# Attention's combining cut finer, two loads doubled earlier, one normalising moved, in a hybrid decoder block on one Trainium2 core

## Chip, cores and metric

One core of one Trainium2 chip runs the whole program. The metric is device time in microseconds (us) of an execution; the figures before are the median of three runs. The engines are TensorE (PE: matmuls; PEld: its weight loads), VectorE (DVE), ScalarE (ACT), GpSimd (POOL) and SyncE (SP), which here only issues DMA transfers.

## The reference

For x of 2048 tokens by 1024 channels, in fp32:

```
h = rmsnorm(x);  proj = h @ w_in                  # q, k, v, u, z, gate_a, gate_b
q, k = rope(q), rope(k);  u, z = gelu(u), gelu(z)
for g in 3 patterns (dilation 1, 4, 16), 4 heads of 64 each:
    o_g, lse_g = windowed attention of 128 keys back
y_attn = sum_g softmax_g(lse) * o_g               # 2048 x 256
y_gmlp = u * (tril(w_spatial) @ layernorm(z) + b) # chunks of 128 tokens, 4 groups
merged = sigmoid(gate_a) * (y_attn @ w_branch_attn) + sigmoid(gate_b) * (y_gmlp @ w_branch_gmlp)
x = x + rmsnorm(merged @ w_out)
h = rmsnorm(x);  x = x + rmsnorm(relu(h @ w_mlp_in)^2 @ w_mlp_out)
```

## The kernel before

Every matmul operand is split into a high part and a remainder, and each product is three matmuls of 128 x 128 by 512 columns (`mm3`); some large products use a seven-product scheme over halves of the operands. Tokens go in chunks c = 0..3 of 512, and in two halves (c = 2, 3 first).

PE's order is the order in which the program is written. The order on the other engines is made by a planner from estimated times; `behind()` pins what is written inside it behind the last instruction written before it on each engine (behind that one only). Each engine then works through its queue in that order, so an instruction that waits holds all that are behind it.

The stretch that the change touches is the middle of the program. A generator (`filler`, advanced by `steps(n)`) gives PE work in steps of three matmuls: the products for u, z and the gates. Around it the code places other work by counting steps.

- `gates()` (line 681) runs the gate products, `seq` of places t, four steps (12 matmuls) each. The last phase (product i = 4 of the first half of tokens) has ten places, from t = LAST; LAST starts at step 34 after the end of attention, LAST+j at step 34 + 4j. At the end of each place the code issues on SP the store of the previous place's result (line 745), then one transfer of the list `ins` (line 748), two at some places, and then evicts the place's PSUM bank with DVE (lines 755 to 769). Four PSUM banks serve the products in turn. In the last phase `ins` holds the operands of the next products: the chunk c = 0 of h (`hT_b`, six 512 KB transfers, of which the first two are rows that ACT and DVE split at LAST+4 and LAST+7, line 716) and the second half of the z weights (`w_z`).
- Attention leaves per pattern an output and its maximum and sum in DRAM (`att_d`). `combine(c)` (line 985) loads the three patterns of a chunk (`A`, three transfers of 528 KB on SP), computes the softmax weights on small tiles (DVE, with one exponential on ACT), multiplies the first pattern's output by its weight (16 small operations on ACT) and the other two (two large products on DVE), adds the three (two large additions on DVE), transposes the sum on PE and stores it (`ya`). It is a generator in five parts. `combined(...)` places the parts of the chunks c = 2, 3, 0 at counted steps during the gate products: loads at steps 0, 4 and 20, weights at 10, 26 and 42, products at 13, 29 and 46, additions at 19, 34 and 49, transposes at 32, 50 and 69. Chunk c = 1 goes through the z products behind (`todo`, line 1116).
- After the gates come the z products of chunks 0 and 1 (`z_chunk`, line 582): eight steps per 128 tokens, a gelu on ACT, statistics on DVE; at the end of a chunk a root on ACT (`rstd_of`, line 103) and four DVE operations that normalise z (line 597).
- Then `load_y` (line 1157) loads the branch operands `yt` (six tiles, split into high part and remainder: four on POOL, two by ACT and DVE, lines 74 and 82), `early_gates` loads gates and the first rows of w_out, and `merge` (line 1197) runs the branch products: 18 matmuls for each of eight dt, evicted by DVE with the gates (line 1211). After dt = 0 and dt = 1 `spatial_out` runs the spatial product of z (`sz`, line 565): chunk 0's after dt = 0, chunk 1's after dt = 1.

Of the kernel before, what the change touches and what calls it, by code (L numbers as in the profile page):

```python
# [9 lines left out]
F32 = mybir.dt.float32  # L10
# [7 lines left out]
P = 128  # L18
# [18 lines left out]
def widen(ap, n):  # L37

    return bass.AP(tensor=ap.tensor, offset=ap.offset, ap=[list(z) for z in ap.ap] + [[0, n]])
# [3 lines left out]
def block_kernel(ctx, tc, a, out):  # L43
# [59 lines left out]
    def rstd_of(pl, ss, n, scale, tag):  # L103

        r = pl.tile([P, n], F32, name=f"r_{tag}", tag=f"rs_r{n}")
        act.activation(r, ss, AF.Sqrt, bias=eps, scale=scale)  # L106
        v = pl.tile([P, n], F32, name=f"v_{tag}", tag=f"rs_v{n}")
        dve.tensor_scalar(v, ss, scale, EPS, op0=OP.mult, op1=OP.add)
        dve.reciprocal(r, r)  # L109
        t = pl.tile([P, n], F32, name=f"t_{tag}", tag=f"rs_t{n}")  # L110
        if n == 1:
            dve.scalar_tensor_tensor(t, r, v, r, op0=OP.mult, op1=OP.mult)  # L112
        else:
            dve.tensor_mul(t, r, r)
            dve.tensor_mul(t, t, v)
        dve.tensor_scalar(t, t, -0.5, 1.5, op0=OP.mult, op1=OP.add)  # L116
        dve.tensor_mul(r, r, t)  # L117
        return r
# [462 lines left out]

    def z_chunk(zp, ws, c):
        zt = zp.tile([P, 4, 512], F32, name=f"z_{c}", tag="z", bufs=2)
        mv = sm.tile([P, 4, 2], F32, name=f"mv_{c}", tag="mv")
        for i in range(4):
            p = psum_mm(f"z_{c}{i}")
            yield from steps_tok(ws, c, i, p)
            if i == 2 and late and c > 1:
                sz_out(*late.pop(0))
            act.activation(zt[:, i, :], p, AF.Gelu_apprx_tanh)  # L590
            bs = sm.tile([P, 6], F32, name=f"bs_{c}{i}", tag="bs")
            dve.bn_stats(bs, zt[:, i, :])
            dve.bn_aggr(mv[:, i, :], bs)
        r = rstd_of(sm, mv[:, :, 1], 4, 1.0, f"ln{c}")
        for i in range(4):
            z = zt[:, i, :]
            dve.tensor_scalar(z, z, mv[:, i, 0:1], r[:, i:i + 1], op0=OP.subtract, op1=OP.mult)
        late.append((zp, zt, c))

    queue = [(9, "u", 0, 1), (10, "u", 1, 1), (11, "z", 0, 1), (12, "z", 1, 1)]  # L600
    queue += [(13, "g", 0, 1)]
    queue += [(11, "z", 0, 0), (12, "z", 1, 0)]
# [78 lines left out]
    def gates():  # L681
# [14 lines left out]
        for t, (half, i, n) in enumerate(seq):  # L696
            if t in starts:
                ph, t0 = starts[t], t
                if ph + 1 < len(phases):
                    s = (ph + 1) % 2  # L700
                    if not slots[s]:
                        slots[s] = hp.tile([P, 2, 2, 4, 512], F32R, name="opA", tag="hT", bufs=2)
                    for j, i2 in enumerate(phases[ph + 1][1]):
                        new = operand(phases[ph + 1][0], i2, slots[s][:, j])
                        ins += new[0]
                        todo += new[1]
                else:
                    hs = reload_h(0)
                    h0 = f32(hT[0])
                    rows = [(h0[:, 1, k:k + 2], hT_d[0][:, k:k + 2]) for k in (0, 2)]  # L710
                    ins += rows + ws[4:6] + hs[4:6] + ws[6:] + hs[6:]
                    todo += [(hT[0], 0), (hT[0], 2)]
            elif todo and (t - t0) % 3 == 1 and t > t0 + 1:
                w, k = todo.pop(0)
                with behind():
                    split(w[:, 0, k:k + 2], w[:, 1, k:k + 2], f32(w)[:, 1, k:k + 2], "act",
                          "pool" if t < LAST else "dve")
            if t == LAST - 4:
                ws = want(5)
                ins += ws[:4]  # L720
            if t == LAST:
                g_["ends"] = g_["vs"] + zs[8:]
            for n_ in (t + PIECES,) if t < LAST else {0: (4, 5), 1: (6, 7), 2: (8,), 3: (9,)}.get(t - LAST, ()):
                piece(n_ if t < LAST else LAST + n_)
            split_piece(t + SPLITS)
            if i in (1, 6, 5, 4):
                bank[n] = psum_mm(f"g{half}{i}{n}")
            p, w, h = bank[n], g_["w"].pop(t), g_["b"][half, i]
            for k in range(4):
                for m, (l, r) in enumerate(((0, 0), (0, 1), (1, 0))):  # L730
                    pe.matmul(p, w[:, l, k], h[:, r, k], start=i in (1, 6, 5, 4) and not k and not m,  # L731
                              stop=k == 3 and m == 2, skip_group_check=True)
                if (t, k) == (3, 2) and late:
                    sz_out(*late.pop(0), zs[4:8])
                yield
            if t == 3:
                a = [ga.tile([P, 512], F32, name=f"ga{n_}", tag=f"ga{n_}", bufs=1) for n_ in range(12)]
                xs += a[:7]
                zs += a[7:9]
                vs = a[9:11]  # L740
                g_["vs"] = vs + xs[8:] + zs[8:]
                g_["raws"] += a[11:]
            x, z, fn = xs[n], zs[n], AF.Copy if n < 8 else AF.Gelu_apprx_tanh
            while out_:
                sp.dma_start(*out_.pop())
            for _ in range(2 if half and i == 4 or t in (LAST + 5, LAST + 7) else 1):
                if ins:
                    sp.dma_start(*ins.pop(0))
            if i == 1:
                act.activation(x, p, AF.Copy)  # L750
            elif i == 2:
                act.activation(z, p, fn)
                o = z, 0, 0
            elif i == 6:
                dve.tensor_add(z, x, p)
            elif i == 7:
                dve.tensor_add(x, x, p)
            elif i == 5:
                if (half, n) == (0, 0):
                    g_["vs"] = a[9:11]  # L760
                v = g_["vs"].pop(0)
                g_["vs"].append(v)
                dve.tensor_add(v, x, p)  # L763
                o = v, 1, 1
            elif i == 3:
                dve.tensor_add(z, z, p)
                o = z, 0, 1
            else:
                dve.tensor_add(x, x, p)
                o = x, 1, 0  # L770
            if n > 7 and i in (5, 3, 4):
                act.activation(o[0], o[0], fn)
            if i in (2, 5, 3, 4):
                c, dst = 2 * half + o[2], gate_d if n < 8 else u_d
                out_.append((dst[n % 8 * 2 + o[1], :, c * 512:(c + 1) * 512], o[0]))
# [209 lines left out]
    def combine(c):  # L985
# [10 lines left out]
        for g in range(3):  # L996
            dve.tensor_sub(E[:, :, g, :], A[:, :, g, 260:264], M)
        act.activation(E, E, AF.Exp, scale=0.125)
        Z = sm.tile([P, 4, 3, 4], F32, name=f"Z_{c}", tag="cZ")
        for g in range(3):  # L1000
            dve.tensor_mul(Z[:, :, g, :], E[:, :, g, :], A[:, :, g, 256:260])
# [3 lines left out]
        for g in range(3):  # L1005
            dve.tensor_mul(E[:, :, g, :], E[:, :, g, :], M)
        yield
        for i in range(4):
            for j in range(4):
                o = A[:, i, 0, j * 64:(j + 1) * 64]  # L1010
                act.activation(o, o, AF.Copy, scale=E[:, i, 0, j:j + 1])
        for g in range(1, 3):
            o = A[:, :, g, 0:256].rearrange("p i (j e) -> p i j e", j=4)
            dve.tensor_tensor(o, o, widen(E[:, :, g, :], 64), op=OP.mult)
        yield
        dve.tensor_add(A[:, :, 1, :256], A[:, :, 1, :256], A[:, :, 2, :256])
        dve.tensor_add(A[:, :, 0, :256], A[:, :, 0, :256], A[:, :, 1, :256])
        yield
        for m in range(2):
# [60 lines left out]
    def combined(*order):  # L1080
        for n, k in order:
            steps(n)
            with behind():
                next(cs[k])

    combined((0, 0), (4, 1), (6, 0), (3, 0), (6, 0), (1, 2), (6, 1), (3, 1), (3, 0), (2, 1),
             (8, 2), (4, 2), (3, 2), (1, 1), (19, 2))
    steps(75 - 69)
    ec.close()
    ega.close()  # L1090
# [22 lines left out]
        steps(1)  # L1113
    for k in range(3):
        load_wb(k)
    todo = {9: (3,), 34: (3,), 36: (3,), 39: (3,), 60: (3,)}
    for n in range(1, 62):
        steps(1)
        if zin:
# [37 lines left out]
    def load_y(c, engs=(("act", "dve"),)):  # L1157
        cs = slice(c * 512, (c + 1) * 512)
        yt = [bot.tile([P, 2, 512], F32R, name=f"yt{c}{k}", tag=f"yt{k}") for k in range(6)]
        for k in range(6):  # L1160
            split_in(yt[k], ya_d[k, :, cs] if k < 2 else yg_d[k - 2, :, cs], None, *engs[k % len(engs)])
        return yt
# [505 lines left out]

    ttp = None
    yt = load_y(2, (("pool", "pool"),) * 4 + (("act", "dve"),) * 2)  # L1670
    early_gates(2)
    mg = merge(2, yt, {}, spatial_out)
    for n, c in enumerate(chunks):
# [414 lines left out]
```

## Time and profile before

| | us |
|---|---|
| median of three runs | 2584.74 (2582.64 to 2586.54) |
| the profiled execution | 2587.89, its span 2586.2 |
| PE busy | 2546.1 |
| DVE busy | 1695.6 |
| POOL busy | 1385.4 |
| ACT busy | 1271.9 |

The profile is of one execution. Its times are counted from the start of the span. A busy PE is not PE at its peak: the time between the starts of two matmuls tells how fast it works, and the granted clock which of its two levels it has. An idle time in brackets names what ended it.

### The profile page before, as it was taken

The numbers are of one execution on the slowest core, as the hardware profiler recorded it, in microseconds if no ns is written. First come the engines' busy times: TensorE is split into PE (matmuls) and PEld (weight loads), VectorE is DVE, ScalarE is ACT, GpSimd is POOL, SyncE is SP. The second block draws the span as 40 slices with busy tenths as digits, with TensorE's granted clock in tenths as the row PEclk, the third lists the DMA queues.
The fourth block names the chain that finished last, engine by engine and source line by source line (L and its number), as shares of the span: only waits on it lengthen the run. The fifth ranks groups of instructions, "written<-read, shape, count | busy, mean of one in ns | idle before, by whom it ended". The sixth has DMA issues, their size and how long they took to land. (4 is left out here: it accounts for less than half of the span.)

```text
span 2586.2 us, 36297 instructions
## 1 busy us (share of the span) xinstructions
PE 2546.1 (98%) x12122; PEld 2125.5 (82%) x12122; DVE 1695.6 (66%) x3063; ACT 1271.9 (49%) x2696; POOL 1385.4 (54%) x1385
## 2 busy tenths in 40 slices
PE   9999999999999999999999999999999999999998
PEld 8888888888888887788887788888778888888886
DVE  5676575445443447777767678778787777767766
ACT  5213211154446434544445645665447776766755
POOL 0363354274545555311113858787887767767634
PEclk9999999999999999999999999999999999999999
DMA  8779778989897899877766766467884222122235
GB/s 313 284 246 325 254 244 278 308 246 296 264 329 218 239 287 326 279 263 266 272 225 240 249 204 212 145 194 215 259 258 143 90 90 89 51 90 90 90 125 201
DMA packets 413293, 568.73 MB, mean 220 GB/s; under 512 B 58929, under 2 KB 247601, under 8 KB 412082
## 3 DMA queue, kind: packets, MB, share of 16 engines
q1 hardware_dynamic: 387600, 504.73, 59.8%
q0 software_dynamic: 15616, 55.06, 5.6%
q10 hardware_dynamic: 9890, 6.62, 0.8%
q8 instruction: 96, 1.57, 0.3%
q14 instruction: 91, 0.75, 0.1%
HBM read 362.16 MB, written 204.14 MB: 219 GB/s over the span
## 5 line engine op out<-in xcount | busy, mean ns | idle before, releaser
L1573 PE MATMUL ha<-spot,hs 128*128 128x512 f32 x1344 | 327.7, 393 | 8.9 <-ACT hs L1351 2.4
L1883 PE MATMUL ya<-spot,s 128*128 128x512 f32 x1344 | 323.2, 389 | 0.0
L1573 PEld LDWEIGHTS ha<-spot,hs 128*128 128x128 f32 x1344 | 253.5, 189 | 65.6 <-ACT sa L1361 3.3
L1883 PEld LDWEIGHTS ya<-spot,s 128*128 128x128 f32 x1344 | 252.3, 188 | 52.3
L1351 ACT ACTIVATE hs<-hraw 128x512 fp32r<-128x512 f32 x168 | 105.0, 626 | 144.3 <-POOL hraw L1412 123.1
L1573 PE MATMUL hc<-spot,hs 128*128 128x512 f32 x672 | 171.1, 390 | 2.6 <-POOL spot L1985 1.7
L731 PE MATMUL g<-opA,spots 128*128 128x512 f32 x672 | 170.5, 398 | 1.8 <-DVE cv L763 1.8
L1883 PE MATMUL yc<-spot,s 128*128 128x512 f32 x672 | 170.5, 389 | 0.0
L731 PE MATMUL g<-opB,spots 128*128 128x512 f32 x648 | 164.0, 397 | 0.0
L1351 ACT ACTIVATE s<-sraw 128x512 fp32r<-128x512 f32 x168 | 104.2, 620 | 108.2 <-POOL sraw L1412 108.2
L1573 PEld LDWEIGHTS hc<-spot,hs 128*128 128x128 f32 x672 | 126.1, 188 | 30.0 <-POOL spot L1985 2.1
L99 PE MATMUL x<-hT_a,wq 128*128 128x512 f32 x384 | 149.7, 390 | 0.0
L101 PE MATMUL x<-hT_a,wq 128*128 128x512 f32 x384 | 149.5, 389 | 0.0
L100 PE MATMUL x<-hT_a,wq 128*128 128x512 f32 x384 | 149.5, 389 | 0.0
L1883 PEld LDWEIGHTS yc<-spot,s 128*128 128x128 f32 x672 | 126.2, 188 | 26.2
L74 ACT ACTIVATE hl<-r 128x512 fp32r<-128x512 f32 x48 | 30.4, 633 | 236.5 <-POOL r L332 89.0
L731 PEld LDWEIGHTS g<-opA,spots 128*128 128x128 f32 x672 | 121.1, 189 | 23.8 <-issue 2.2
L82 POOL TENSOR_TENSOR spots<-gr,spots 128x512 fp32r<-128x512 f32 x98 | 128.4, 1314 | 22.3 <-DMA gr<-in_w_in_dram 7.9
L1744 ACT ACTIVATE sraw<-sraw 128x1024 f32<-128x1024 f32 x128 | 133.9, 1046 | 2.4 <-DMA sraw<-sd 2.3
L731 PEld LDWEIGHTS g<-opB,spots 128*128 128x128 f32 x648 | 116.9, 189 | 21.1
L76 POOL TENSOR_SCALAR spots<-gr 128x512 fp32r<-128x512 f32 x86 | 55.4, 644 | 131.9 <-PE g L731 97.0
L981 DVE TENSOR_REDUCE o<-po 128x256 f32<-128x512 f32 x48 | 33.2, 692 | 133.9 <-PE po L980 133.9
(471 smaller groups left out, 6844.7 us busy)
## 6 DMA issues: line engine op xcount, KB each, us to landing
sraw<-sd SPq DMA_DIRECT2D x128, 256.0 KB, 3.3
qk<-hl SPq DMA_DIRECT2D x24, 1024.0 KB, 5.7
qq<-qk SPq DMA_DIRECT2D x96, 256.0 KB, 5.4
sd<-e SPq DMA_DIRECT2D x64, 256.0 KB, 3.6
hraw<-wsd SPq DMA_DIRECT2D x32, 512.0 KB, 4.6
w2r<-in_w_mlp_out_dram SPq DMA_DIRECT2D x16, 1024.0 KB, 9.2
g<-gated SPq DMA_DIRECT2D x56, 256.0 KB, 5.5
gr<-sgd SPq DMA_DIRECT2D x53, 256.0 KB, 5.0
```

The costliest lines, as they stand in the source:

```text
L74: act.activation(hi, src, AF.Copy)
L76: pool.tensor_scalar(hi, src, 1.0, 1.0, op0=OP.mult, op1=OP.mult)
L82: (pool if lo_eng == "pool" else dve).tensor_sub(lo, src, f32(hi))
L99: pe.matmul(ps, lh, rh, start=start, stop=False)
L100: pe.matmul(ps, lh, rl, start=False, stop=False)
L101: pe.matmul(ps, ll, rh, start=False, stop=stop)
L731: pe.matmul(p, w[:, l, k], h[:, r, k], start=i in (1, 6, 5, 4) and not k and not m, stop=k == 3 and m == 2, skip_group_check=True)
L981: dve.tensor_reduce(ot[:, :, j * 64:(j + 1) * 64], po.rearrange("p (b h e) -> p b e h", b=4, h=2), axis=AX.X, op=OP.add)
L1351: act.activation(hi, src, AF.Copy)
L1573: pe.matmul(p, w[:, l, S_AT[i], kk * P:(kk + 1) * P], b[r], start=i in (1, 2, 5) and not kk and not z, stop=kk == 1 and z == 2, skip_group ...
L1744: act.activation(sraw_[n], sraw_[n], func)
L1883: pe.matmul(p, s[:, l], w[r], start=i in (1, 2, 5) and not m and not o, stop=m == 1 and o == 2, skip_group_check=True)
```

## The change

The combining of a chunk gets seven parts behind its load in place of four, each three steps behind the one before; the load of c = 0's patterns is at step 46 and its parts at steps 49 to 64; the transposes are at steps 33, 51 and 69. In the last gate phase the places with two transfers are LAST+1, LAST+3 and LAST+5 instead of LAST+5 and LAST+7. Chunk 1's normalising is written behind `load_y`, its small tiles in the pool that stays open until then.

```diff
     def z_chunk(zp, ws, c):
         zt = zp.tile([P, 4, 512], F32, name=f"z_{c}", tag="z", bufs=2)
-        mv = sm.tile([P, 4, 2], F32, name=f"mv_{c}", tag="mv")
+        kept = zp if c == 1 else sm
+        mv = kept.tile([P, 4, 2], F32, name=f"mv_{c}", tag="mv")
...
-        r = rstd_of(sm, mv[:, :, 1], 4, 1.0, f"ln{c}")
-        for i in range(4):
-            z = zt[:, i, :]
-            dve.tensor_scalar(z, z, mv[:, i, 0:1], r[:, i:i + 1], op0=OP.subtract, op1=OP.mult)
+
+        def normalise():
+            r = rstd_of(kept, mv[:, :, 1], 4, 1.0, f"ln{c}")
+            for i in range(4):
+                z = zt[:, i, :]
+                dve.tensor_scalar(z, z, mv[:, i, 0:1], r[:, i:i + 1], op0=OP.subtract, op1=OP.mult)
+
+        if c == 1:
+            unnormed.append(normalise)
+        else:
+            normalise()
         late.append((zp, zt, c))
...
-            for _ in range(2 if half and i == 4 or t in (LAST + 5, LAST + 7) else 1):
+            for _ in range(2 if half and i == 4 or t in (LAST + 1, LAST + 3, LAST + 5) else 1):
                 if ins:
                     sp.dma_start(*ins.pop(0))
...
         act.activation(E, E, AF.Exp, scale=0.125)
+        yield
         Z = sm.tile([P, 4, 3, 4], F32, name=f"Z_{c}", tag="cZ")
...
-        for i in range(4):
-            for j in range(4):
-                o = A[:, i, 0, j * 64:(j + 1) * 64]
-                act.activation(o, o, AF.Copy, scale=E[:, i, 0, j:j + 1])
         for g in range(1, 3):
+            for i in range(2 * g - 2, 2 * g):
+                for j in range(4):
+                    o = A[:, i, 0, j * 64:(j + 1) * 64]
+                    act.activation(o, o, AF.Copy, scale=E[:, i, 0, j:j + 1])
             o = A[:, :, g, 0:256].rearrange("p i (j e) -> p i j e", j=4)
             dve.tensor_tensor(o, o, widen(E[:, :, g, :], 64), op=OP.mult)
-        yield
+            yield
         dve.tensor_add(A[:, :, 1, :256], A[:, :, 1, :256], A[:, :, 2, :256])
+        yield
         dve.tensor_add(A[:, :, 0, :256], A[:, :, 0, :256], A[:, :, 1, :256])
         yield
...
-    combined((0, 0), (4, 1), (6, 0), (3, 0), (6, 0), (1, 2), (6, 1), (3, 1), (3, 0), (2, 1),
-             (8, 2), (4, 2), (3, 2), (1, 1), (19, 2))
+    places = [(0, 0), (4, 1), (46, 2)]
+    places += [(13 + 18 * k + 3 * n, k) for k in range(3) for n in range(6)]
+    places += [(33, 0), (51, 1), (69, 2)]
+    at_step = 0
+    for step, k in sorted(places):
+        combined((step - at_step, k))
+        at_step = step
...
-    todo = {9: (3,), 34: (3,), 36: (3,), 39: (3,), 60: (3,)}
+    todo = {n: (3,) for n in (9, 34, 35, 36, 38, 40, 42, 60)}
...
     yt = load_y(2, (("pool", "pool"),) * 4 + (("act", "dve"),) * 2)
+    unnormed.pop()()
     early_gates(2)
```

## Rows read from the trace of the kernel before

**Rows 1.** The page, busy time of PE: us, share of the span, instructions.

```profile
PE 2546.1 (98%) x12122; PEld 2125.5 (82%) x12122; DVE 1695.6 (66%) x3063; ACT 1271.9 (49%) x2696; POOL 1385.4 (54%) x1385
```

**Rows 2.** PE's waits: who waited for whom, us in total, times, longest us.

```profile
PE z L99 <- DMA hT_b<-hbd: 3.2, 1, 3.2
...
PE b L100 <- DVE yt L82: 2.5, 1, 2.5
...
PE g L731 <- DVE cv L763: 1.8, 1, 1.8
...
PE b L99 <- DVE gates L1211: 0.7, 1, 0.7
```

**Rows 3.** PE's timeline, gate products: start, us, instruction, count, [idle before <-releaser].

```profile
957.40 20.70 PE L731 MATMUL g<-opA,spots 128*128 128x512 f32 x90
979.90 1.62 PE L731 MATMUL g<-opA,spots 128*128 128x512 f32 x6 [1.79 <-DVE cv L763]
...
1008.32 1.03 PE L1022 MATMUL yt<-ident,A 128*128 128x128 f32 x8
```

**Rows 4.** PE's timeline at the first z products; then a stretch with its granted clock.

```profile
1012.61 0.39 PE L99 MATMUL z<-w_z,hT_b 128*128 128x512 f32 x1
...
1016.46 0.39 PE L101 MATMUL z<-w_z,hT_b 128*128 128x512 f32 x1
...
1026.42 0.39 PE L101 MATMUL z<-w_z,hT_b 128*128 128x512 f32 x1
...
1020.00:1026.00 6.00, 5.75 (x13) 4.07 (x14) 0.88 (x2) 0.60 (x1) 0.00 (x0) 0.50 0.95 314
```

**Rows 5.** Timelines of PE, DVE and ACT where the branch products begin.

```profile
1067.50 0.49 PE L99 MATMUL b<-yt,wb 128*128 128x512 f32 x1
...
1072.84 4.19 PE L565 MATMUL sz<-wsp,z 128*128 128x128 f32 x32
...
1080.96 3.73 PE L565 MATMUL sz<-wsp,z 128*128 128x128 f32 x32
...
1067.97 1.91 DVE L597 TENSOR_SCALAR z<-z,mv,r_ln 128x512 f32<-128x512 f32 x4
1069.80 1.29 DVE L82 TENSOR_TENSOR yt<-yt 128x512 fp32r<-128x512 f32 x2
...
1066.84 1.13 ACT L74 ACTIVATE yt<-yt 128x512 fp32r<-128x512 f32 x2
```

**Rows 6.** Stretches: us, busy PE, PEld, DVE, ACT, POOL (instructions), PE clock, DMA share, GB/s.

```profile
967.50:1010.20 42.70, 40.91 (x193) 33.84 (x192) 41.05 (x70) 25.02 (x67) 30.72 (x24) 1.00 0.93 310
983.00:991.00 8.00, 8.00 (x37) 6.64 (x36) 7.90 (x9) 7.29 (x21) 7.75 (x5) 1.00 0.52 159
```

**Rows 7.** DVE's timeline: combining of the chunks, evictions and splits between.

```profile
967.53 0.20 DVE L993 TENSOR_TENSOR M<-A 128x16 f32<-128x16 f32 x1 [2.30 <-DMA A<-att]
...
979.07 0.68 DVE L763 TENSOR_TENSOR cv<-ga,g 128x512 f32<-128x512 f32 x1
...
983.13 3.87 DVE L1014 TENSOR_TENSOR A<-A,E 128x1024 f32<-128x1024 f32 x2
...
989.35 1.45 DVE L1017 TENSOR_TENSOR A<-A 128x1024 f32<-128x1024 f32 x1
...
1003.58 1.45 DVE L1017 TENSOR_TENSOR A<-A 128x1024 f32<-128x1024 f32 x1
...
1008.39 1.82 DVE L82 TENSOR_TENSOR hT_b<-hT_b 128x1024 fp32r<-128x1024 f32 x1
...
1051.18 1.22 DVE L1014 TENSOR_TENSOR cw<-cw,E 128x1024 f32<-128x1024 f32 x1
```

**Rows 8.** SP's timeline (issue of transfers); then tile A, 957 to 1012: issue to landing.

```profile
968.73 4.47 SPq L990 DMA_DIRECT2D A<-att x3
...
1011.20 2.36 SPq L748 DMA_DIRECT2D hT_b<-hbd x2
...
DMA to landing us min/median/max: 4.5/9.5/10.5
```

**Rows 9.** DVE's timeline in the merge.

```profile
1073.15 0.69 DVE L1211 TENSOR_TENSOR gates<-gates,b 128x512 f32<-128x512 f32 x1 [1.46 <-PE b L101]
1074.38 0.75 DVE L575 SCALAR_TENSOR_TENSOR sb<-sz,lngb,bsp 128x512 f32<-128x512 f32 x1 [0.55 <-PE sz L565]
...
1104.67 1.22 DVE L82 TENSOR_TENSOR wo<-woraw,wo 128x1024 fp32r<-128x1024 f32 x1 [2.27 <-ACT wo L74]
```

More of the change, by code (lines that the diff above doesn't have):

```diff
@@ L593, in z_chunk @@
             dve.bn_aggr(mv[:, i, :], bs)
-        r = rstd_of(sm, mv[:, :, 1], 4, 1.0, f"ln{c}")
-        for i in range(4):
-            z = zt[:, i, :]
-            dve.tensor_scalar(z, z, mv[:, i, 0:1], r[:, i:i + 1], op0=OP.subtract, op1=OP.mult)
+        def normalise():
[7 more added lines that the diff above has]
+            normalise()
         late.append((zp, zt, c))
+    unnormed = []
     queue = [(9, "u", 0, 1), (10, "u", 1, 1), (11, "z", 0, 1), (12, "z", 1, 1)]
@@ L1007, in combine @@
         yield
-        for i in range(4):
-            for j in range(4):
-                o = A[:, i, 0, j * 64:(j + 1) * 64]
-                act.activation(o, o, AF.Copy, scale=E[:, i, 0, j:j + 1])
         for g in range(1, 3):
+            for i in range(2 * g - 2, 2 * g):
+                for j in range(4):
+                    o = A[:, i, 0, j * 64:(j + 1) * 64]
+                    act.activation(o, o, AF.Copy, scale=E[:, i, 0, j:j + 1])
             o = A[:, :, g, 0:256].rearrange("p i (j e) -> p i j e", j=4)
             dve.tensor_tensor(o, o, widen(E[:, :, g, :], 64), op=OP.mult)
+            yield
+        dve.tensor_add(A[:, :, 1, :256], A[:, :, 1, :256], A[:, :, 2, :256])
         yield
-        dve.tensor_add(A[:, :, 1, :256], A[:, :, 1, :256], A[:, :, 2, :256])
         dve.tensor_add(A[:, :, 0, :256], A[:, :, 0, :256], A[:, :, 1, :256])
```

## The prediction

> **What bounds the kernel now.** I read the page's busy times first: PE is busy 2546.1 of 2586.2 us [rows 1], so nothing but the 40 us in which TensorE (PE) stands, and the matmuls that run slow after such a stop, can be won. The list of PE's waits comes next [rows 2]: it names no long wait, only single ones, and three of them lie where the diff works: 3.2 us for a load of `hT_b`, 2.5 us for a branch operand `yt`, 1.8 us for VectorE's (DVE's) eviction into `cv`. Then PE's timeline at these three places, since a stop costs more than its idle time.
>
> A matmul of 512 columns starts every 0.2265 us at full clock: 17 of them lie between 1012.61 and 1016.46 [rows 4]. With that:
> - `cv`: 90 matmuls from 957.40 would end at 977.80; the next starts at 979.90 [rows 3]. Loss 2.1 us. No slow clock follows.
> - `hT_b`: between 1016.46 and 1026.42 lie 15 starts, worth 3.4 us; they took 9.96 us. Loss 6.6 us: 3.2 idle, the rest the clock, granted at 0.50, that is 1.2 instead of 2.4 GHz, from 1020 to 1026 [rows 4].
> - `yt`: 1067.50 to 1072.84 holds 6 starts, 1.36 us, and took 5.34; the 32 small `sz` matmuls behind it took 4.19 us, the next 32 only 3.73 [rows 5]. Loss 4.4 us, again with a slow clock.
> With the 0.7 us for `gates` at 1107 [rows 2] this makes 13.8 us, the pool that this change can draw on.
>
> What stands behind the first two is DVE. From 967.5 to 1010.2 it is busy 41.05 of 42.70 us [rows 6]; SP's stores wait for its evictions and SP's loads wait behind these stores. The last two loads of `hT_b` are issued at 1011.20 [rows 8], after which they need some 7 to 9 us.
>
> **The change, part by part.**
>
> *Loads two at a time.* At 1011.20 SP issues both last `hT_b` loads, behind the store of t = LAST+6. In the new order the last of them goes at LAST+6 and the one before at LAST+5, each behind one store fewer or two: a period is 12 matmuls, 2.7 us, so 2.7 and 5.4 us earlier by the code, and they were 3.2 us late. No instruction is added. I take the wait as gone: gain 6.6 us; the bounds are 6.6 and 0 (if the DMA engines and not the issue are the limit: they are busy 0.93 of these 43 us [rows 6]).
>
> *Combining at even places.* Three chunks go through DVE here (the fourth in the z phase, where ScalarE (ACT) and DVE have room; cost 0, at worst some tenths, since its transposes stay at step 60). Instructions are the same in number; only their places move. ACT's sixteen small products of a chunk go eight and eight, and it is busy 25 of these 42.7 us [rows 6]: cost 0. For the first chunk the evictions get between its parts. The late eviction at 979.07 [rows 7] stands behind everything of chunk one but its last addition, and 0.7 us of chunk two's first part; the latter goes to step 31, behind it. I take 1.1 us off the 2.1 us stall (bounds 0 and 2.1).
>
> The third chunk is where I expect a new wait. Its parts move from steps 42, 46, 49 to 49, 52, ..., 64, while the transposes that need the result stay at step 69 in PE's written order. Before, its last addition ran at 1003.58 to 1005.03 [rows 7] and PE came to the transposes at 1008.32 [rows 3]: 20 steps (13.6 us) of distance had shrunk to 3.3 us, because DVE lags. Now add what gets ahead of that addition: it is pinned behind the second split of `hT_b`, which is pinned behind the eviction of LAST+6. So all work that DVE had done at 1008.39 + 1.82 = 1010.2 must be done first. DVE begins it at 967.53 [rows 7] as before, as the first A lands no earlier, and it had only 1.65 us of idle time in it. PE gets to step 69 at 1008.3 less the 1.1 us won: 1007.2. That is a stop of 3.0 us by mere conservation of work.
>
> Then the load of the third A moves from step 20 (issued 968.73) to step 46. Nine such loads took 9.5 us from issue to landing in the middle, 4.5 at least, 10.5 at most [rows 8]. It can't be issued before the store of LAST's eviction, at about 988 (983.6 + 2.7 us of matmuls, and DVE's lag); so it lands between 992.5 and 998.5, and I take 997, near the middle value, since the queue is full there by then. On SP its three issues (4.47 us [rows 8]) now stand ahead of LAST+1's store, of the rest of `w_z` and of the four `hT_b` loads: these can go up to 4.5 us later than the code alone says; the stop below covers it. DVE would be through with chunk two at about 993 (in the old order its last addition ended at 990.8 [rows 7], with two evictions fewer before it). Less one eviction of 0.7 us that fits in, 3.3 us of standing DVE. Against it: GpSimd (POOL) is not slowed in this time. Two products of chunk two took 3.87 us together while POOL was busy 7.75 of 8 us, one alone 1.22 [rows 6, 7]; so some 1.8 us are given back. Moving the 1.6 MB also empties the DMA queue at 969 to 983 and fills it after 988; between 983 and 991 the DMA engines were busy only 0.52 [rows 6], which takes most of it. Stop at step 69: 3.0 + 3.3 - 1.8 = 4.5 us; bounds 0 (DVE's operations shortened throughout, as the single product shows) and 10.5 (A not before 1003, as in the rival below).
>
> The Trainium skill, SBUF — State Buffer, Who interferes with whom, says that a DVE instruction with two SBUF inputs contends with a GpSimd instruction that reads SBUF. Rows 6 and 7 agree (1.22 against 1.9 us each); by this rule spreading the products over more of POOL's splits helps nothing, and the 1.8 us given back would be 0, the stop 6.3 us.
>
> A stop of 4.5 us is longer than both that brought the half clock (2.5 and 3.2 us), so this one brings it too: 4.4 - 2.8 = 1.6 us at the smaller, 6.6 - 3.2 = 3.4 at the larger; I take 2.1, nearer to the smaller, as 1.8 us of idle brought none. The new wait costs 6.6 us, as much as the `hT_b` wait that it replaces; and with it PE comes to z late enough that those loads are surely there.
>
> *Normalising behind the branch operands.* Now ACT loads a table and computes the root, DVE normalises from 1067.97 for 1.91 us, and only then splits `yt` at 1069.80 [rows 5]. After the change ACT's two copies come right behind the last gelu (about 1065.3) and end at 1066.5, DVE's two subtractions (1.29 us) follow the statistics at 1066.3 and end at 1067.6. PE needs them at 1067.25 + 0.2 and 1068.1: no stop. The normalised chunk is used by the second `sz` block (1080.96, then about 1076.6 [rows 5]); it is ready at some 1071.1. Gain 4.4 us. What is late next: the evictions and weights of the merge. PE already waited 0.7 us for `gates`, behind a split of `wo` that waited for ACT [rows 9]. DVE wins only the 1.46 and 0.55 us that it waited for PE at 1073 and 1074 [rows 9], less 0.1 for the later normalising, so the merge's chain comes 1.9 us earlier and PE 4.4: 2.5 us go back. Net 1.9 (bounds 4.4 and -0.5: all of it back, with a slow clock).
>
> **Sum.** -1.1 - 6.6 + 6.6 - 1.9 = -3.0 us. The profiled execution took 2587.89 us, 3.15 over the median of the three runs shown; it gives 2584.9 us, and on the median 2584.74 - 3.0 = 2581.7 us.
>
> **The rivals.**
> *The clean gain.* DVE keeps up and step 69 doesn't wait. For it: DVE's times are swollen by POOL, and the first loads of the phase come sooner, so POOL may be ahead. Against it: the 1.65 us of slack. Without the 6.6 us: 2575.1 us.
> *The late A.* The third A lands so late that DVE stands for long: its M is at the head of DVE's queue, behind it the evictions, behind these SP's stores and loads. For it: landing took up to 10.5 us [rows 8], and the three issues alone can take 4.5. Each us beyond 997 costs one us at step 69, and the clock up to 1.3 more: at 999 it is even with before, at 1003 it gives 2581.7 + 6 + 1.3 = 2589.0 us. Against it: the DMA engines have room at 983 to 991.
> *The change doesn't do what it says.* If the transfers are the limit and not their issue, the earlier loads land as late as before, and z waits as now; with 1.1 + 1.9 us won and up to 4 us for the A that now runs in the same stretch: 2582 to 2586, say 2584 us. For it: DMA share 0.93; against it the gap at 983.
>
> **How the numbers follow.** My forecast (stops swapped, range 2578 to 2585) 0.48; clean gain 0.26; late A 0.16; loads no earlier 0.10. 0.2% is 5.2 us: faster means below 2579.6, slower above 2589.9; less than that a measurement of this kernel can hardly tell. Faster: 0.24 of the clean gain, 0.12 of my own case: 0.36. Slower: 0.10 of the late A, 0.04 of the others: 0.14. The same: 0.50. Range 2575 to 2589.
>
> **What would show it.** Right: in PE's list of waits `z <- hT_b`, `g <- cv` (or shorter than 1.2) and `b <- yt` are gone, and there stands a wait of `yt <- A` (the transposes) for DVE of 3 to 7 us near 1007, with the half clock behind it; DVE waits 2 to 5 us for `A` near 994; waits for `gates` in the merge sum to 2 to 4 us. Wrong: no wait at the transposes (clean gain), or the `hT_b` wait still there, or transposes of the first two chunks waiting; the third part is wrong if `sz` waits for z, or if the merge's waits don't grow.

## The result and the profile after

The changed kernel takes 2592.32 us (median of 8 runs, 2591.44 to 2595.46) against 2584.81 us (8 runs, 2582.64 to 2588.22) beside it on the same chip: ratio 1.0032, interval 1.0023 to 1.0041. It is slower by 7.5 us, where 3 us less were forecast. The profiled execution took 2591.44 us (span 2589.7), 3.55 us more than the profiled one of before, which lay 3.1 us above its own median; the accounts below are of these two executions and explain 3.55 us, not the whole 7.5.

The first view is the list of PE's waits of the changed kernel from 860 to 1200 us (who waited for whom, us in total, times, longest us), to be held against [rows 2].

```profile
PE yt L1033 <- DVE A L1028: 9.3, 1, 9.3
PE b L100 <- DVE yt L82: 2.5, 1, 2.5
PE g L740 <- DVE cv L772: 1.1, 1, 1.1
```

The `hT_b` wait is gone, as forecast. The `cv` wait went from 1.8 to 1.1 us. The `yt` wait of the branch, which the third part should have taken away, is there unchanged. And the transposes of the last chunk wait 9.3 us, where 4.5 were forecast. PE's timeline at these places (start, us, instruction, count, [idle before <-releaser]), for [rows 3 to 5]:

```profile
956.77 20.70 PE L740 MATMUL g<-opA,spots 128*128 128x512 f32 x90
978.59 2.31 PE L740 MATMUL g<-opA,spots 128*128 128x512 f32 x9 [1.12 <-DVE cv L772]
...
994.66 12.50 PE L740 MATMUL g<-opB,spots 128*128 128x512 f32 x54
1016.46 1.94 PE L1033 MATMUL yt<-ident,A 128*128 128x128 f32 x8 [9.29 <-DVE A L1028]
...
1018.05 5.31 PE L740 MATMUL g<-opB,spots 128*128 128x512 f32 x15
1023.20 0.40 PE L99 MATMUL z<-w_z,hT_b 128*128 128x512 f32 x1
...
1030.46 0.39 PE L101 MATMUL z<-w_z,hT_b 128*128 128x512 f32 x1
...
1074.55 0.50 PE L100 MATMUL b<-yt,wb 128*128 128x512 f32 x1 [2.55 <-DVE yt L82]
...
1075.81 3.73 PE L565 MATMUL sz<-wsp,z 128*128 128x128 f32 x32
```

The same instruction's start, before and after, gives the account:

| instruction | before | after | difference |
|---|---|---|---|
| gate product behind the `cv` wait | 979.90 | 978.59 | -1.3 |
| first z product | 1012.61 | 1023.20 | +10.6 |
| z product behind the `hT_b` wait of before | 1026.42 | 1030.46 | +4.0 |
| first `sz` | 1072.84 | 1075.81 | +3.0 |
| end of the span | 2586.2 | 2589.7 | +3.5 |

The stop at the transposes costs 11.9 us by this table: 9.3 of idle, and most of the rest since PE takes 6.7 us instead of 4.3 from the transposes to the first z product, at the lower clock (granted 0.67 from 1015 to 1025). The missing `hT_b` wait gives back 6.6. At the branch 1.0 us is won although the wait is as long as before, since its matmuls go on at full clock (0.50 us for the first where the kernel before took 0.80, shown in the last section).

DVE's queue shows where the stop comes from (same columns; this answers to [rows 7]):

```profile
994.03 0.68 DVE L778 TENSOR_TENSOR ga<-ga,g 128x512 f32<-128x512 f32 x1
1000.40 0.18 DVE L1002 TENSOR_TENSOR M<-A 128x16 f32<-128x16 f32 x1 [5.70 <-DMA A<-att]
1000.49 0.68 DVE L778 TENSOR_TENSOR ga<-ga,g 128x512 f32<-128x512 f32 x1
1002.80 0.18 DVE L1003 TENSOR_TENSOR M<-M,A 128x16 f32<-128x16 f32 x1 [1.62 <-DMA A<-att]
...
1013.84 1.23 DVE L82 TENSOR_TENSOR hT_b<-hT_b 128x1024 fp32r<-128x1024 f32 x1 [0.73 <-ACT hT_b L74]
1014.98 1.22 DVE L1028 TENSOR_TENSOR A<-A 128x1024 f32<-128x1024 f32 x1
```

DVE stands 7.3 us for the third A, in two waits at the head of its queue; its last addition ends at 1016.2, the transposes start at 1016.46. The whole stretch from its first maximum to that addition (us, then busy PE, PEld, DVE, ACT, POOL with their instructions, clock, DMA share, GB/s), to be held against [rows 6]:

```profile
967.01:1016.20 49.19, 39.03 (x180) 31.86 (x178) 38.69 (x70) 23.86 (x65) 27.66 (x24) 0.95 0.96 330
```

For as many instructions as in the kernel before DVE is busy 38.69 us instead of 41.05, but it stands 10.5 us instead of 1.65. SP's queue (issues), and the transfers of tile A between 986 and 1004, for [rows 8]:

```profile
989.46 0.32 SPq L757 DMA_DIRECT2D w_z<-wzd  x1
991.70 0.37 SPq L655 DMA_DIRECT2D ga<-sgd  x1
992.12 3.18 SPq L999 DMA_DIRECT2D A<-att  x3
...
DMA to landing us min/median/max: 6.0/6.8/7.9
```

The transfers took less than was reckoned (6.0 to 7.9 us, not 9), but they were issued from 992.1 to 995.3, not at 988. The load of `ga` ahead of them was issued only at 991.70, 1.9 us after SP was through with the issue before it; what held it is not shown.

### The profile page after: what moved, and what is told of

It reads as the page before. It is cut to its first block, busy times and chain, and to the rows that moved or that the text cites. A ratio compares the mean times of both kernels' runs of the same rounds, so it can differ in the third digit from the quotient of the medians.

```text
span 2589.7 us, 36293 instructions
## 1 busy us (share of the span) xinstructions
PE 2540.8 (98%) x12122; PEld 2120.8 (82%) x12122; DVE 1691.7 (65%) x3063; ACT 1272.7 (49%) x2696; POOL 1384.1 (53%) x1385
```

## The experiments

All ratios are to the kernel before, run beside them. Two causes were on trial for the stop: the late landing of the third A, and the places (the work that DVE must do ahead of the last addition, with the transposes left at step 69). Beside them stood the question whether the other two parts do what they say.

**The third load back at step 20.**

```diff
-    places = [(0, 0), (4, 1), (46, 2)]
+    places = [(0, 0), (4, 1), (20, 2)]
```

> The changed kernel with one edit: the third chunk's A is loaded at step 20 again, not at step 46; its parts stay at 49 to 64. Theory (the late load is most of the cost): DVE's two waits for that A (5.7 and 1.6 us) go, the transposes at step 69 wait 2 to 4 us instead of 9.3 (what is left is work that DVE has to do ahead of the last addition), 2584 to 2587 us, that is 6 to 8 us off the changed kernel. Rival (the late places of the parts are the cost, whatever the load): the transposes still wait 7 us or more, 2590 us or more. Second rival: with the wait gone z waits for hT_b again, 2588 us.

Measured: 2587.65 us, ratio 1.0010 [1.0001, 1.0018]. So the late load is 0.22% of the time, some 5.7 us (with some 3 us of uncertainty, as each ratio carries 0.09% either way), but half of the stop stays. PE's waits, and DVE's queue (columns as above) with a row of the stretch in which DVE must be through:

```profile
PE yt L1033 <- DVE A L1028: 4.7, 1, 4.7
...
998.17 1.86 DVE L1011 TENSOR_TENSOR Z<-E,A 128x16 f32<-128x16 f32 x3
...
1000.15 1.26 DVE L1013 TENSOR_TENSOR M<-M,Z 128x16 f32<-128x16 f32 x1
...
1009.46 1.22 DVE L1028 TENSOR_TENSOR A<-A 128x1024 f32<-128x1024 f32 x1
...
965.86:1010.70 44.84, 39.03 (x179) 31.57 (x177) 41.67 (x70) 23.88 (x65) 26.85 (x23) 1.00 0.97 331
```

From its first maximum on DVE waits for no load here. Up to the last addition it is busy 41.67 us, where the kernel before had 41.05 [rows 6] and the forecast took 1.8 off, and stands 3.2 instead of 1.65. The third chunk's last addition did get shorter (1.22 us against 1.45 [rows 7]), but small operations ahead of it did not: three of 128x16 took 1.86 us, and one 1.26. In the changed kernel, where DVE stands for the late A, it is busy 3.0 us less over the same work, so part of that standing is given back.

**Before, with the earlier pairs of loads alone.**

```diff
-... t in (LAST + 5, LAST + 7) else 1):
+... t in (LAST + 1, LAST + 3, LAST + 5) else 1):
```

> The kernel before with the two-at-a-time loads alone (LAST+1, LAST+3, LAST+5). Theory (issue is the limit): z's wait for hT_b goes or falls under 1 us, no half clock there, 3 to 6 us faster than before, 2579 to 2582 us. Rival (the DMA engines are the limit): the loads are issued earlier and land as before, z waits 2 to 3 us, within 1.5 us of before.

Measured: 2583.34 us, ratio 0.9988 [0.9979, 0.9997], some 3 us. The wait, and the stretch around it (columns as above):

```profile
PE z L101 <- DMA hT_b<-hbd: 0.3, 1, 0.3
...
1015.00:1025.00 10.00, 9.72 (x43) 7.75 (x42) 1.31 (x3) 1.20 (x2) 0.57 (x3) 1.00 1.01 345
```

The `hT_b` wait is 0.3 us and no half clock follows (granted 1.00): the part does what it says.

**Before, with the normalising behind the branch operands in the engines' order too.** In the changed kernel it is written behind `load_y`, but DVE's and ACT's queues have it where they had it:

```profile
1069.34 1.28 ACT L106 ACT_TABLE_LOAD   x1
1070.63 0.30 ACT L106 ACTIVATE r_ln<-mv,edge 128x4 f32<-128x4 f32 x1
1070.84 1.13 ACT L74 ACTIVATE yt<-yt 128x512 fp32r<-128x512 f32 x2
...
1071.97 1.92 DVE L600 TENSOR_SCALAR z<-z,mv,r_ln 128x512 f32<-128x512 f32 x4
1073.80 1.29 DVE L82 TENSOR_TENSOR yt<-yt 128x512 fp32r<-128x512 f32 x2
```

This is the order of [rows 5], each row 4.0 us later. So a pin was added:

```diff
     yt = load_y(2, ...)
+    with behind():
+        unnormed.pop()()
```

> The kernel before with the normalising of chunk 1 alone moved, and pinned behind the last split of yt on DVE and ACT, so that it cannot run ahead of it. Theory (the forecast's third part holds once the order is really changed): the 2.5 us wait for yt goes, the merge's waits for gates grow from 0.7 to 2 to 4 us, 1 to 3 us faster, 2582 to 2584 us. Rival: it all goes back in the merge, within 1 us of before. Other rival: nothing goes back, 4 us faster.

Measured: 2588.41 us, ratio 1.0008 [0.9999, 1.0017]. The wait is gone, the first `sz` comes at 1064.74 (8.1 us before the kernel before, 3.8 of which it had ahead of the branch already, at the z product of 1026.42, now 1022.58). PE's waits in the merge:

```profile
PE b L99 <- DVE g L1221: 2.2, 1, 2.2
...
PE b L99 <- DVE gates L1221: 2.1, 1, 2.1
...
PE sz L565 <- DVE sb L575: 0.7, 1, 0.7
```

The branch product that waited for `gates` at 1107.15 [rows 2] stands at 1105.55: of 8.1 us 1.6 are left, so the merge takes 6.5 us for the 4.3 that the pin won.

**Before, with the third load at step 41 instead of 20**, its parts unchanged.

```diff
-    combined(..., (6, 0), (1, 2), (6, 1), (3, 1), (3, 0), (2, 1), (8, 2), ...)
+    combined(..., (6, 0), (7, 1), (3, 1), (3, 0), (2, 1), (7, 2), (1, 2), ...)
```

> The kernel before with one edit: the third chunk's A is loaded at step 41, not 20, just ahead of its first part at 42. Theory (late load): DVE waits 3 to 6 us for it near 993, the transposes at step 69 wait 1 to 5 us and z waits 3 us or more for hT_b, as SP's loads are held too; 4 to 9 us slower than before, 2589 to 2594 us. Rival (DVE's order and pins make the cost, not the load): within 2 us of before.

Measured: 2585.53 us, ratio 0.9999 [0.9990, 1.0008]. DVE waits 4.8 us for A, and yet nothing is lost, where the same load cost 0.22% in the changed kernel; PE stops 0.8 us at the transposes. DVE's queue, then PE's second stop for `hT_b`:

```profile
1000.29 0.18 DVE L993 TENSOR_TENSOR M<-A 128x16 f32<-128x16 f32 x1 [4.78 <-DMA A<-att]
...
1009.38 1.45 DVE L1017 TENSOR_TENSOR A<-A 128x1024 f32<-128x1024 f32 x1
1010.75 1.27 DVE L769 TENSOR_TENSOR ga<-ga,g 128x512 f32<-128x512 f32 x2
1011.95 2.35 DVE L82 TENSOR_TENSOR hT_b<-hT_b 128x1024 fp32r<-128x1024 f32 x2
...
1022.62 0.50 PE L101 MATMUL z<-w_z,hT_b 128*128 128x512 f32 x1 [1.88 <-DMA hT_b<-hbd]
```

Here two evictions and both splits of `hT_b` stand behind the last addition; in the changed kernel they stand ahead of it. PE comes to the transposes at 1010.93, 2.6 us later than the kernel before (1.5 of them had gathered up to `cv`), and the wait for `hT_b` behind them takes that up: 2.4 us in two stops instead of 3.4, and no half clock behind it. So the late load by itself is not the cause: at the transposes it costs only what the place of the reader leaves uncovered, and here a stop that stood behind anyway hid even that. That gave the next question: is it the distance between the last addition and the transposes, or DVE's sum of work?

**Load at step 20 and the transposes at 75.**

```diff
-    places += [(33, 0), (51, 1), (69, 2)]
+    places += [(33, 0), (51, 1), (75, 2)]
```

> The changed kernel with the third chunk's operands loaded at step 20 (as in the run before it) and, besides, that chunk's transposes placed at step 75 of the phase and not at 69, behind three more groups of 18 products. Theory (TensorE stops at the transposes because they are asked for at one place of its queue while VectorE's queue reaches the last addition later): the 4.7 us wait of the run with the load at step 20 goes to under 1 us, and 2582 to 2584 us is left, the time of the kernel with the loads alone. Rival (VectorE's sum of work between the phase's second half and z's products is the bound, wherever the transposes stand): the wait goes over to z's products, whose operand halves VectorE splits in the same stretch, and the time stays at 2586 to 2588.

Measured: 2581.81 us, ratio 0.9982 [0.9973, 0.9990]: the fastest version, and faster than the kernel before. The waits, and PE at the transposes:

```profile
PE yt L1033 <- DVE A L1028: 1.3, 1, 1.3
...
1011.35 1.06 PE L1033 MATMUL yt<-ident,A 128*128 128x128 f32 x8 [1.32 <-DVE A L1028]
```

Fifteen more products stand ahead of the transposes, and DVE is reached when it is nearly through. No half clock follows (1.06 us for the eight, not 1.94). Of the 3.4 us 0.6 came back, as a wait of a z product for `hT_b` at 1039.9.

**The transposes at 75 with the late load.**

> The changed kernel as it is, its third load at step 46, with the third chunk's transposes at step 75 and not at 69. If the late landing and the early place of the transposes add up, the wait of 9.3 us goes to about 5 us (six steps further on are about 4.1 us of products) and the time to 2588 to 2590; if the late landing by itself is what costs, the time stays at 2591 to 2592.

Measured: 2588.8 us, ratio 1.0011 [1.0002, 1.0020], a stop of 4.9 us. The four kernels make a square: load late and place 69, 1.0032; late and 75, 1.0011; early and 69, 1.0010; early and 75, 0.9982. Either edit is worth 0.21 to 0.29%, whichever way the other stands: both causes are real, and within the intervals they add up.

**Load at step 20, the third chunk's parts seven steps earlier.**

```diff
-    places += [(13 + 18 * k + 3 * n, k) for k in range(3) for n in range(6)]
+    places += [(13 + 18 * k + 3 * n - 7 * (k == 2), k) for k in range(3) for n in range(6)]
```

> The changed kernel with the third load at step 20 and the third chunk's six parts seven steps earlier each (steps 42 to 57 and not 49 to 64), its transposes at step 69 as in the change. Theory (distance between the last addition and its reader in VectorE's queue): the second split of the branch weights and some copies of products now stand behind the last addition, the wait at the transposes is 0 to 1.5 us and the time 2582 to 2584. Rival (VectorE's whole work is late, and the order of its pieces is of no matter): the wait stays over 3 us, or comes back at z's products as a wait for the weight halves, and the time stays at 2586 to 2588.

Measured: 2588.46 us, ratio 1.0012 [1.0003, 1.0021]. A miss: the wait left the third chunk's transposes and came to the second's, which neither theory had said. PE, then DVE:

```profile
997.82 1.94 PE L1033 MATMUL yt<-ident,A 128*128 128x128 f32 x8 [6.04 <-DMA ga<-sgd]
...
996.35 1.21 DVE L1028 TENSOR_TENSOR A<-A 128x1024 f32<-128x1024 f32 x1
```

The profile names a load as the releaser, but the second chunk's last addition ended at 997.56, just ahead of the transposes; it was pushed back by the third chunk's first parts.

**Load at step 20, the remainders of `hT_b` on POOL.**

```diff
-                          "pool" if t < LAST else "dve")
+                          "pool")
```

> The changed kernel with the third load at step 20 and the two remainder halves of the branch weights formed on GpSimd and not on VectorE, where each took about 1.2 to 1.5 us ahead of the last addition. Theory (VectorE's work ahead of the last addition sets the stop): the 4.7 us wait goes to 1.5 to 2.5 us and the time to 2584 to 2586. Rival: GpSimd is late with its share, and z's products wait for the halves instead; the time stays at 2587 or grows.

Measured: 2587.74 us, ratio 1.0006 [0.9997, 1.0016]; the stop is 5.0 us, not shorter. DVE lost two instructions (2.8 us in the run with the load at step 20) and yet was busy 42.10 us up to its last addition, against 41.67. That addition ran beside POOL's split:

```profile
1007.92 2.77 DVE L1028 TENSOR_TENSOR A<-A 128x1024 f32<-128x1024 f32 x1
...
1006.28 3.33 POOL L82 TENSOR_TENSOR hT_b<-hT_b 128x1024 fp32r<-128x1024 f32 x1
```

It took 2.77 us where it took 1.22 in the run without it, and the two products ahead of it 3.47 instead of 2.36. This is the rule of the Trainium skill, SBUF — State Buffer, Who interferes with whom, that a DVE instruction with two SBUF inputs contends with a GpSimd instruction that reads SBUF; the trace agrees. The work was not taken from DVE but came back to it as longer operations.

**The fastest version with the pin.**

> The changed kernel with its third load at step 20 and the third chunk's transposes at step 75 (2581.81 us, ratio 0.9982, with a 2.2 us wait for the last branch operand), and the last chunk's normalising held behind the branch operands in VectorE's order, not only written behind them. Theory (what the pin gains at the branch's start is lost in the merge, since the spatial products' later results let the loads of u and behind them the fourth load of the out-weights start later, as in the pinned run on the kernel before): the 2.2 us wait is gone, new waits of 2 to 5 us in all stand between 1075 and 1105, and the time is that of the kernel without the pin, 2581 to 2583.5. Rival (the loss in the merge belonged to the kernel before and its half-speed stretch): 2577 to 2580.

Measured: 2586.57 us, ratio 1.0001 [0.9992, 1.0010], that is 0.19% behind the version without the pin; neither the theory's no change nor the rival's gain. The first `sz` comes 4.7 us earlier than without it (1063.47 against 1068.16), the branch product of 1102.25 comes 1.3 us later (1103.50). DVE, POOL:

```profile
1083.62 1.46 DVE L579 TENSOR_TENSOR sb<-sb,ur 128x512 f32<-128x512 f32 x1 [1.91 <-DMA ur<-ud]
1085.00 0.68 DVE L1227 TENSOR_TENSOR gates<-gates,b 128x512 f32<-128x512 f32 x1
...
1083.27 2.95 POOL L579 TENSOR_TENSOR sb<-sb,ur 128x512 f32<-128x512 f32 x2 [7.01 <-DMA ur<-ud]
1086.16 1.65 POOL L1166 DMA_DIRECT2D woraw<-in_w_out_dram  x3
```

PE waits 2.65 us up to 1085.73 for that eviction of `gates`. In the pinned order a product that needs a late load (`ur`) stands ahead of it on DVE, and ahead of three loads of w_out on POOL. This stop, with the slow clock behind it (granted 0.64 to 1090.5), takes 4.3 of the 6 us that are lost up to 1103.50; two shorter waits (0.55 and 1.43 us) take most of the rest. Another 2.4 us are lost between there and the end of the profiled execution; they were not followed. That the late `ur` is the cause is read from the trace; no run took it away.

**The fastest version with the loads as before** (one at a time; of the change only the seven parts).

> The same kernel (third load at step 20, third chunk's transposes at step 75, no pin) with the operand loads one at a time as before, so that of the change only the seven parts are left. Theory (the branch weights' loads stand behind the operand loads in SP's queue, and start about 3 us later when these go out one at a time): the z products wait 2 to 4.5 us for the last half of the weights, some of it followed by products at half speed, and the time is 2584 to 2587. Rival (with the third chunk's load at step 20 the queue is free by then and the pairs are of no use): no wait there, 2581 to 2583.

Measured: 2581.93 us, ratio 0.9985 [0.9976, 0.9994]. The theory falls: with the third A early and the transposes at 75 nothing waits for `hT_b`, and the pairs bring nothing. Alone they bring 0.12%, the seven parts at good places 0.15%, both together 0.18%: they take away one and the same wait, and no two of the three can be told apart by these intervals.

## Why the prediction was wrong

- **Loads two at a time:** the wait went, -6.6 us forecast and seen, and by itself the part does it (the run with the loads alone). In the changed kernel, though, PE comes to the product that waited up to 1020.01 in the kernel before only at 1027.29, behind the stop at the transposes; the loads of the kernel before, which were there by 1021.47, would have done as well. So the 6.6 us are seen, but not shown to come from the pairs there.
- **The late `cv`:** 1.1 us forecast, 0.7 seen (90 products from 956.77 end at 977.17, the next starts at 978.59: a loss of 1.4 instead of 2.1).
- **The stop at the transposes:** right as a mechanism, and wrong in size: 6.6 us with its clock were forecast, 11.9 seen. This is the step that failed: the term "3.0 + 3.3 - 1.8 = 4.5 us" came out at 9.3. DVE's row in the changed kernel says in which part. The 1.8 us of shorter operations came, and more (38.69 us busy instead of 41.05); DVE's standing time was mis-sized. For the third A it stands 7.3 us, where 3.3 were reckoned, and otherwise 3.2, where the 1.65 of before were kept: 4.0 + 1.5 - 0.6 is 4.9, for the 4.8 that were missing. On A, the prediction put the issue at the earliest moment that the code allows, "about 988"; SP came to it at 992.1, behind a load of `w_z` and one of `ga`, and to the third transfer some 3 us later. The duration, on which the prediction spent its rows, was overrated.
- **What the run with the load at step 20 adds:** without the late A the stop is 4.7 us, so the late A costs 4.6 of the 9.3, and "3.0 - 1.8 = 1.2 us" for DVE's own work and place was 4.7. In that run none of the 1.8 us came (DVE busy 41.67 us, 0.6 more and not less), and it stands 1.5 us longer than before; 1.8 + 0.6 + 1.5 is 3.9, for the 3.5 that were missing. So the shorter operations of the changed kernel came with the late A and not from the finer parts, and for these the bound that the prediction worked out by the rule of the Trainium skill (SBUF — State Buffer, Who interferes with whom), that spreading the products "helps nothing", was the better value.
- **Two sums of the prediction:** of the 1.8 us its rows show 1.4 (3.87 - 2 x 1.22), and the clock's price at the smaller stop is 4.4 - 2.5 = 1.9 us, not 4.4 - 2.8 = 1.6. Neither changes the account.
- **Normalising:** wrong. It was taken for granted that the order written is the order run. Without a pin DVE and ACT kept theirs, and a gain of 1.9 us was booked for an edit that changes nothing there. With the pin the gain at the branch comes (4.3 us, 4.4 forecast) and the merge takes 6.5, 2.2 more than all of it, where the prediction's lower bound was -0.5 ("all of it back, with a slow clock").
- **The sum:** -3.0 forecast; 3.55 us slower by the two profiled executions. The misses are 5.3 us at the stop and 0.4 at `cv`. At the branch and in the merge up to 1107.15 (now 1108.85) 2.3 us were won instead of 1.9, which is luck and not the mechanism booked: a clock that did not fall and a `gates` wait of 0.7 us that went. Ahead of the changed stretch the profiled run was 0.6 us quicker. Behind 1107, where nothing was changed, it lost 1.9 us net, in single stops that differ either way, among them 1.9 us of waiting for `g` at 1346 that the kernel before had not, 1.7 us won at 1384 by a clock that did not fall behind the same 2.0 us of waiting, 2.0 us lost at 1411 by one that did. The medians differ by 7.5 us; the 4 us that these two executions do not show are not settled.
- **The rivals:** the late A was the nearest, with A landing at 1003 (the last small wait for it ended at 1002.80) and 2589.0 us. It got 0.16. With DVE's own work reckoned at 4.7 us instead of 1.2 it comes to 2592.5 us (2589.0 + 3.5); that this meets the median of 2592.32 is in part luck, since it still counts the 1.9 us of the normalising, and 4 us of that median are unexplained.

## What to carry to other kernels

A load's landing is its place in the issuing queue plus the transfer: count what SP must issue ahead of it, and what those issues wait for, before taking the earliest moment that the code allows. When work on a busy engine is spread later, move the place where its result is read as well; a square of the two edits (early or late load, early or late reader) costs four runs and shows which of them pays. And a moved line is not a moved instruction where something else makes the queues' order: look whether the order must change before a gain is booked.

## What was not expected of the hardware

The length of a stop does not tell by itself whether the clock falls. At the same place, 2.5 us of idle brought the half clock in the kernel before (the next matmul took 0.80 us; granted 0.50 from 1071.0 to 1072.8), and 2.55 us did not in the changed kernel (0.50 us; granted 1.00 from 1074.5 to 1075.8). 2.20 us brought it in the fastest version, and the same 2.20 us did not in the kernel before with the earlier pairs of loads. Before, fastest version, earlier pairs:

```profile
1070.54 0.80 PE L100 MATMUL b<-yt,wb 128*128 128x512 f32 x1 [2.54 <-DVE yt L82]
...
1065.86 0.80 PE L100 MATMUL b<-yt,wb 128*128 128x512 f32 x1 [2.20 <-DVE yt L82]
...
1064.61 0.50 PE L100 MATMUL b<-yt,wb 128*128 128x512 f32 x1 [2.20 <-DVE yt L82]
```

Nothing that PE did just ahead differs between the kernel before and the changed one: the same matmuls at the same distances. What decides is not in these rows. Of the ten kernels that stop here, for 2.20 to 2.55 us, eight got the half clock and two did not. The stops at the transposes of 4.7 us and more all brought it, those of 1.3 us none. From the first matmul ahead of it to the first `sz` the stop cost 3.0 us in the changed kernel (1071.50 to 1075.81, for 1.36 us of matmuls) and 4.0 in the kernel before, whose `sz` then lost another 0.4: a forecast should carry both prices.
